# Cutting the weights of the closing products of a triangular inverse to the columns that are used

## Chip, cores and metric

The kernel runs on one core of a Trainium2 chip. The metric is the device time of one execution in microseconds, the median of the runs; the profiled execution is one further run of the same program.

## What is computed

One layer of a hybrid encoder over a prompt of 1024 tokens and a sample of 512. Half of it is a gated delta rule with 8 heads, run once forwards and once backwards over the tokens; the other half is latent attention. The delta rule works in chunks, and within a chunk it solves a unit triangular system:

```python
L = jnp.where(strict, jnp.einsum('bhnid,bhnjd->bhnij', kb, k) * decay, 0.0)
A = L + jnp.eye(CHUNK, dtype=L.dtype)
u = lax.linalg.triangular_solve(A, v * beta[..., None], left_side=True, lower=True, unit_diagonal=True)
w = lax.linalg.triangular_solve(A, kb * jnp.exp(gc)[..., None], left_side=True, lower=True, unit_diagonal=True)
```

After the scan over chunks the two directions are added, normalised and gated; a projection joins both halves, and a norm and the residual close the layer.

## The kernel before

It uses chunks of 128 tokens and forms the inverse of each chunk's triangular matrix explicitly, once per head, chunk and direction. There are 12 jobs: 8 for the prompt (one head, 8 chunks) and 4 for the sample (two heads, 4 chunks each), so 8 slots in each job, times two directions.

A job goes through three generators. `gdn_front` (from line 641) loads keys and queries, forms the decays (`dec`, L673) and the products of keys (`kk`, L681), and writes the strict triangles and the attention weights into the tile `UA` (L686). Its four 32x32 diagonal blocks per slot are inverted by substitution on VectorE, 31 steps of a product and a subtraction (`tm` L737, `XT` L739), and go through DRAM (`dX`) to be spread into block-diagonal matrices.

`gdn_back` (from line 747) reads them back as `dds`, transposes them (`Dp`, L762), so that `Dt` holds the block-diagonal inverse, and multiplies the triangle with it (`Fp`, L773); ScalarE copies the product into the tile `F`. Three rounds follow (lines 780 to 795) which close the inverse from blocks of 32 to 128: `Tt = Dt - F^T Tt`. The first round takes all of the columns; the second takes the 64 columns, and the third the 32 columns, that are not final yet. `cs` are the columns that are computed and `ms` the partitions (rows of the result) that change; which end of the tile they are at depends on the direction. L793 subtracts the partitions `ms` alone. A group is four slots of each direction, so that a round issues eight products, direction 0 first, and a job has two groups. An f32 product appears in the trace as two loads of weights and two matmuls.

`gdn_scan` (from line 799) then carries the state over the chunks: `pk` (L832, L835), `py` (L854), `pu` (L870, L873), with `oacc` (L844, L847, L888) collecting the output.

These generators run as streams beside others: the input projection of the sample (`mm`, L224 to L228), then the preparation of the attention (`pq`), then the attention itself (`s`, `pt`, `po`). `merge` (line 136) interleaves them on TensorE in an order fixed by hand: each stream yields a due time in a clock that `self.cost` (line 116) advances, and the first stream that is due goes next. `cost` is charged with the moving columns of a product, not with its weights. `free` and `hold` keep the PSUM banks of the two directions (`h0`, `h1`) apart in the same clock. The order on the other engines comes from the framework's planner at build time (`schedule_with_timeline_sim`, line 1377), and SyncE issues the DMAs in its own queue.

Of the kernel before, what the change touches and what calls it, by code (L numbers as in the profile page):

```python
# [57 lines left out]
class Kern:  # L58
# [688 lines left out]
    def gdn_back(self, turn, q, T, heads, env, KQ, UA):  # L747

        nc, (gp, cp, psc, dds, dXs) = self.nc, env
        dX = dXs[turn % 2]  # L750
        for items in (((0, 0), (1, 4)), ((0, 4), (1, 0))):
            Ds = {}
            for d, g0 in items:
                src = dX[d].rearrange("(n b) w -> n (b w)", b=4)[g0:g0 + 4, :P * P]
                nc.sync.dma_start(dds[d], src.rearrange("n (r c) -> r n c", c=P))
            yield self.t + 4
            yield from self.free(0, 1)
            for d, g0 in items:
                dd = dds[d]
                ps = psc.tile([P, 4, P], F32, tag=f"h{d}", name="Dp")  # L760
                for i in range(4):
                    nc.tensor.transpose(ps[:, i], dd[:, i], self.ident)  # L762
                    self.cost(P, 2)
                dt2 = cp.tile([P, 4, P], F32, tag="dt2", name="dt2", bufs=2)
                nc.scalar.copy(dt2, ps)
                Ds[d] = (dt2, dd) if d == 0 else (dd, dt2)
            self.hold(HT, 0, 1)
            yield self.t + self.tlat
            yield from self.free(0, 1)
            for d, g0 in items:  # L770
                ps = psc.tile([P, 4, P], F32, tag=f"h{d}", name="Fp")
                for i in range(4):
                    nc.tensor.matmul(ps[:, i], UA[:, d, g0 + i, 0], Ds[d][0][:, i], start=True, stop=True)  # L773
                    self.cost(P, 4)
                F = cp.tile([P, 4, P], F32, tag="F", name="F", bufs=2)
                nc.scalar.copy(F, ps)
                Ds[d] += (F,)
            self.hold(HT, 0, 1)
            yield self.t + self.tlat
            for it, lo in enumerate((0, 64, 96)):  # L780
                yield from self.free(0, 1)
                for d, g0 in items:
                    _, Dt, F = Ds[d]
                    Tt = UA[:, d, g0:g0 + 4, 0]

                    far, near = slice(lo, P), slice(0, P - lo)
                    cs, ms = (far, near) if d == 0 else (near, far)
                    cur = Dt if it == 0 else Tt
                    ps = psc.tile([P, 4, P - lo], F32, tag=f"h{d}", name="Tp")
                    for i in range(4):  # L790
                        nc.tensor.matmul(ps[:, i], F[:, i], cur[:, i, cs], start=True, stop=True)  # L791
                        self.cost(P - lo, 4)
                    nc.vector.tensor_sub(Tt[ms, :, cs], Dt[ms, :, cs], ps[ms])  # L793
                self.hold(HT, 0, 1)
                yield self.t + self.tlat
            if g0 == 4:
                yield
# [595 lines left out]
```

## Time and profile before

| what | value |
|---|---|
| time, median of 3 runs | 3361.96 us |
| lowest and highest run | 3359.56 and 3369.88 us |
| profiled execution: time | 3363.58 us |
| profiled execution: span | 3361.7 us |
| TensorE products, weight loads busy | 3212.2 and 2688.5 us |
| VectorE, ScalarE, GpSimd busy | 1735.1, 1283.6 and 1158.5 us |

The span is the time from the first to the last instruction of the profiled execution. PE stands for TensorE's products, PEld for its loads of weights, which run under the product before; DVE is VectorE, ACT ScalarE, POOL GpSimd, SP SyncE. A product's record is longer than its share of the engine, since products are pipelined: what one costs in a row of many is seen from the distance between starts, or from the chain of work, where each piece ends as the next begins. A form such as 128*32 128x64 gives the rows and columns of weights in use, then the partitions and moving columns.

### The profile page before, as it was taken

Reading aid. Unit: us, or ns where it says so; the run is one execution under the profiler, and the core shown is the slowest. Engines: PE = TensorE matmul, PEld = TensorE weight load, DVE = VectorE, ACT = ScalarE, POOL = GpSimd, SP = SyncE. Lnnn points to the kernel's source line nnn. Section 1 sums busy time; section 2 is a strip of 40 time slices with the busy share of each in tenths; the row PEclk is TensorE's granted clock in tenths of the full one; section 3 lists DMA queues with packets and bytes.
Section 4 is the critical chain, followed back from the end, with each engine's and each line's share of the span. In section 5 each row is a group of like instructions: output and inputs, shape, how many; then the busy total and the mean of one; then the engine's idle time right before and its main releaser. Section 6 shows DMA issues by size and latency. Waiting matters only on the chain.

```text
span 3361.7 us, 46959 instructions
## 1 busy us (share of the span) xinstructions
PE 3212.2 (96%) x16554; PEld 2688.5 (80%) x16554; DVE 1735.1 (52%) x4000; ACT 1283.6 (38%) x2956; POOL 1158.5 (34%) x1026
## 2 busy tenths in 40 slices
PE   8999999999999899999999989899999989999998
PEld 6888888888887688788788777688898878787876
DVE  7234333443412656774775577688787655331212
ACT  4222222222212334444345334365656555432231
POOL 6322222222223532332332334222222444464452
PEclk9999999999999899999999999899999999999999
DMA  4222222222223534334433466522222242564454
GB/s 159 83 73 79 72 78 75 78 72 79 84 75 105 159 100 126 116 107 129 131 111 120 135 211 206 155 82 70 89 76 64 99 135 86 155 186 135 143 168 135
DMA packets 271404, 381.66 MB, mean 114 GB/s; under 512 B 75632, under 2 KB 126824, under 8 KB 269632
## 3 DMA queue, kind: packets, MB, share of 16 engines
q1 hardware_dynamic: 271168, 378.66, 37.0%
q8 instruction: 130, 2.13, 0.3%
q14 instruction: 106, 0.87, 0.1%
HBM read 286.73 MB, written 88.29 MB: 112 GB/s over the span
## 4 chain that ended last, share of the span: by engine, by line
PE 65%; DVE 15%; DMA 10%; issue 3%; ACT 3%; POOL 2%; SPq 1%; POOLq 0%; DVEq 0%; ACTq 0%
PE mm L224 13%; PE mm L228 12%; PE mm L225 12%; DMA wraw<-w_out 3%; PE py L1152 3%; PE py L1151 3%; PE py L1153 3%; DVE tm L737 3%; DVE XT L739 2%; PE Tp L791 2%; POOL wlo L199 2%; PE pt L1074 2%; DMA wraw<-w_in 1%; DVE UA L686 1%; DVE acc L306 1%
## 5 line engine op out<-in xcount | busy, mean ns | idle before, releaser
L199 POOL TENSOR_TENSOR wlo<-wraw,whi 128x512 fp32r<-128x512 f32 x620 | 832.3, 1346 | 1610.4 <-ACT whi L196 1522.3
L224 PE MATMUL mm<-hi,whi 128*128 128x512 f32 x2256 | 910.6, 405 | 16.9 <-ACT whi L196 11.7
L225 PE MATMUL mm<-lo,whi 128*128 128x512 f32 x2256 | 884.7, 393 | 8.1 <-DVE lo L255 8.1
L196 ACT ACTIVATE whi<-wraw 128x512 fp32r<-128x512 f32 x620 | 389.0, 631 | 1181.5 <-PE mm L225 693.4
L228 PE MATMUL mm<-hi,wlo 128*128 128x512 f32 x2256 | 767.5, 394 | 1.6 <-POOL wlo L199 1.5
L224 PEld LDWEIGHTS mm<-hi,whi 128*128 128x128 f32 x2256 | 429.3, 190 | 101.1 <-ACT whi L196 13.7
L228 PEld LDWEIGHTS mm<-hi,wlo 128*128 128x128 f32 x2256 | 427.7, 190 | 97.1 <-POOL wlo L199 5.0
L225 PEld LDWEIGHTS mm<-lo,whi 128*128 128x128 f32 x2256 | 429.4, 190 | 92.7 <-DVE lo L255 10.0
L1151 PE MATMUL py<-whi,mhi 128*128 128x512 f32 x768 | 304.1, 396 | 9.9 <-DVE y L1166 5.6
L1152 PE MATMUL py<-wlo,mhi 128*128 128x512 f32 x768 | 303.8, 396 | 7.5 <-POOL wlo L199 7.4
L1153 PE MATMUL py<-whi,mlo 128*128 128x512 f32 x768 | 302.8, 394 | 0.0
L1035 POOL TENSOR_TENSOR pe<-pe,af 128x512 f32<-128x512 f32 x160 | 166.8, 1060 | 377.8 <-DVE af L1033 203.9
L306 DVE SCALAR_TENSOR_TENSOR acc<-cin,conv_w,acc 128x1024 f32<-128x1024 f32 (+1 forms) x192 | 219.3, 1142 | 40.8 <-ACT acc L304 33.2
L302 DVE TENSOR_TENSOR cin<-mm,rbh 128x512 f32<-128x512 f32 x72 | 47.4, 687 | 311.6 <-PE mm L228 262.6
L1151 PEld LDWEIGHTS py<-whi,mhi 128*128 128x128 f32 x768 | 145.1, 189 | 45.4 <-DVE y L1166 7.5
L1152 PEld LDWEIGHTS py<-wlo,mhi 128*128 128x128 f32 x768 | 145.2, 189 | 44.3 <-POOL wlo L199 12.8
L1153 PEld LDWEIGHTS py<-whi,mlo 128*128 128x128 f32 x768 | 144.8, 189 | 32.3
L310 DVE TENSOR_TENSOR acc<-mm,rbh 128x512 f32<-128x512 f32 x48 | 31.6, 686 | 231.3 <-PE mm L228 231.3
L1166 DVE TENSOR_TENSOR y<-py,g 128x512 f32<-128x512 f32 x36 | 24.7, 690 | 239.1 <-ACT junk L1165 235.7
L1021 ACT ACTIVATE pe<-s,am 128x512 f32<-128x512 f32 x160 | 110.5, 691 | 92.7 <-DVE am L1020 85.6
L737 DVE TENSOR_TENSOR tm<-XT,lam 128x126 f32<-128x126 f32 (+22 forms) x372 | 128.8, 346 | 23.2 <-ACT lam L729 16.1
L199 DVE TENSOR_TENSOR ptl<-pt,pth 128x512 fp32r<-128x512 f32 x160 | 109.9, 687 | 56.9 <-ACT pth L196 55.8
(449 smaller groups left out, 5251.9 us busy)
## 6 DMA issues: line engine op xcount, KB each, us to landing
wraw<-w_in SPq DMA_DIRECT2D x376, 256.0 KB
wraw<-w_out SPq DMA_DIRECT2D x192, 256.0 KB
dd<-dX SPq DMA_DIRECT2D x48, 256.0 KB
wraw<-w_uq SPq DMA_DIRECT2D x36, 256.0 KB
x<-xT_p SPq DMA_DIRECT2D x16, 512.0 KB
xres<-x_p SPq DMA_DIRECT2D x8, 1024.0 KB
y_p<-y SPq DMA_DIRECT2D x32, 256.0 KB
x<-xT_s SPq DMA_DIRECT2D x16, 256.0 KB
```

The lines of the kernel that those rows point to most:

```text
L196: nc.scalar.activation(hi, src, AF.Copy)
L199: (lo_eng or nc.vector).tensor_sub(lo, src, hi.bitcast(F32))
L224: nc.tensor.matmul(ps, whi[:, k], hi[:, s], start=kt == 0, stop=False)
L225: nc.tensor.matmul(ps, whi[:, k], lo[:, s], start=False, stop=False)
L228: nc.tensor.matmul(ps, wlo[:, k], hi[:, s], start=False, stop=kt == KT - 1)
L306: nc.vector.scalar_tensor_tensor(acc, cin[:, j:j + T], w[:, f, j:j + 1], acc, op0=ALU.mult, op1=ALU.add)
L737: nc.vector.tensor_mul(tv, XT[:, :m, j:j + 1].to_broadcast([P, m, n]), lam[j // 16][:, j % 16:j % 16 + 1, j + 1:].to_broadcast([P, m, n]))
L1021: nc.scalar.activation(pe[k], o, AF.Exp, bias=m[:, k:k + 1], scale=-1.0, accum_out=l[:, k:k + 1])
L1035: nc.gpsimd.tensor_mul(pe[k2], pe[k2], f[:, k2:k2 + 1].to_broadcast([P, BLK]))
L1151: nc.tensor.matmul(ps, hi[:, c], w[0], start=kt == kts[0], stop=False)
L1152: nc.tensor.matmul(ps, hi[:, c], w[1], start=False, stop=False)
L1153: nc.tensor.matmul(ps, lo[:, c], w[0], start=False, stop=kt == kts[1] - 1)
```

## The change

The product of the closing rounds takes from `F` only those columns of weights whose results L793 reads, and writes only those partitions of PSUM.

```diff
                     ps = psc.tile([P, 4, P - lo], F32, tag=f"h{d}", name="Tp")
                     for i in range(4):
-                        nc.tensor.matmul(ps[:, i], F[:, i], cur[:, i, cs], start=True, stop=True)
+                        nc.tensor.matmul(ps[ms, i], F[:, i, ms], cur[:, i, cs], start=True, stop=True)
                         self.cost(P - lo, 4)
                     nc.vector.tensor_sub(Tt[ms, :, cs], Dt[ms, :, cs], ps[ms])
```

In the first round `lo` is 0 and `ms` is the whole tile. In the second `ms` has 64 partitions, in the third 32: from partition 0 on for direction 0, and the last ones of the 128 for direction 1.

## Rows read from the trace of the kernel before

**Rows 1.** The page's first part: busy time, share of the span, instructions.
```profile
PE 3212.2 (96%) x16554; PEld 2688.5 (80%) x16554; DVE 1735.1 (52%) x4000; ACT 1283.6 (38%) x2956; POOL 1158.5 (34%) x1026
```

**Rows 2.** Table by stretches: length, busy us and instructions of each engine, clock.
```profile
core 0: us, PE busy (x) PEld busy (x) DVE busy (x) ACT busy (x) POOL busy (x), PEclk, DMA share, GB/s
1200.00:2525.00 1325.00, 1253.91 (x7455) 1076.76 (x7454) 931.45 (x2591) 613.93 (x1676) 409.31 (x395) 0.98 0.41 122
```

**Rows 3.** TensorE's waits from 1200 to 2525 us: total, times, longest.
```profile
PE pk L832 <- DVE oacc L888: 10.5, 9, 3.8
PE py L854 <- DVE oacc L844: 8.8, 12, 2.2
PE py L854 <- ACT oacc L847: 8.1, 9, 2.4
PE pt L1074 <- DVE ptl L199: 5.6, 7, 2.0
PE Fp L773 <- ACT dt L765: 5.1, 2, 3.5
```

**Rows 4.** The chain that ended last, 1200 to 2525 us: shares of the stretch.
```profile
by line: DVE tm L737 6.1%; PE mm L224 5.5%; PE mm L228 5.4%; PE mm L225 5.4%; PE Tp L791 5.3%; DVE XT L739 5.3%; issue 3.8%; DMA wraw<-w_in 2.8%; DVE UA L686 2.5%; DVE acc L306 2.2%; PE Fp L773 1.9%; PE kk L681 1.9%; PE py L854 1.8%; PE pt 
```

**Rows 5.** Groups by line and form, L791: busy us, mean ns | idle before.
```profile
L791 PEld LDWEIGHTS Tp<-UA,F 128*128 128x128 f32 x768 | 91.7, 192 | 4.1 <-DVE z L919 1.1 <-ACT dec L673 0.4 <-DVE UA L793 0.2
L791 PE MATMUL Tp<-UA,F 128*128 128x64 f32 x384 | 45.8, 272 | 0.1
L791 PE MATMUL Tp<-UA,F 128*128 128x32 f32 x384 | 44.9, 271 | 0.7 <-DVE z L919 0.7
```

**Rows 6.** Chain in order of time: start us, us, what; rounds one, two, three.
```profile
1305.09 1.79 PE Tp L791 x16
...
1309.83 1.73 PE Tp L791 x16
...
1314.39 1.71 PE Tp L791 x16
1316.09 0.31 PE mm L224
```

**Rows 7.** Groups by line and form: loads of weights for transposes.
```profile
L762 PEld LDWEIGHTS Dp<-ident,dd 128*128 128x128 f32 x192 | 22.2, 140 | 2.5
...
L491 PEld LDWEIGHTS gtps<-ident,gz 128*32 128x32 f32 x12 | 1.1, 95 | 4.2 <-ACT egls L482 3.0 <-POOL gz L489 0.5
...
L400 PEld LDWEIGHTS crow<-ident,cy 128*8 128x8 f32 x2 | 0.2, 84 | 0.1
```

**Rows 8.** Chain in order of time: products of keys, 256 moving columns.
```profile
1212.71 1.73 PE kk L681 x8
```

**Rows 9.** Timeline of TensorE, four transposes of 64 columns: start us, us, what.
```profile
87.44 0.32 PEld L439 LDWEIGHTS abps<-ident,cacc 64*128 64x128 f32 x4 [0.37 <-issue]
```

**Rows 10.** Timeline of TensorE, and the chain at that time.
```profile
1222.19 1.86 PE L791 MATMUL Tp<-UA,F 128*128 128x32 f32 x16
...
1222.04 1.35 DVE acc L306
```

**Rows 11.** Timeline of TensorE around the transpose into `qcols`.
```profile
889.47 0.61 PE L228 MATMUL mm<-hi,wlo 128*128 128x512 f32 x2
890.02 0.13 PEld L363 LDWEIGHTS qcols<-ident,qrows 64*128 64x128 f32 x1 [0.35 <-issue]
...
890.56 0.40 PE L225 MATMUL mm<-lo,whi 128*128 128x512 f32 x1
```

**Rows 12.** Timeline of TensorE around the transposes into `gtps`.
```profile
117.65 0.39 PE L225 MATMUL mm<-lo,whi 128*128 128x512 f32 x1
117.66 0.32 PEld L491 LDWEIGHTS gtps<-ident,gz 128*32 128x32 f32 x2
117.88 0.38 PE L491 MATMUL gtps<-ident,gz 128*32 128x128 f32 x2
...
118.33 0.40 PE L225 MATMUL mm<-lo,whi 128*128 128x512 f32 x1
```

## What I predict

> **What bounds the kernel now.** I read the shares of the engines first. TensorE's products fill 96% of the span, VectorE 52%, ScalarE 38%, GpSimd 34% [rows 1]. TensorE is the first suspect, but a share averages over stages. So the second view is the table by stretches, cut where the line of the change begins and ends its work: L791 runs from 1201 to 2525 us. In those 1325 us TensorE is busy 1253.9 us, so 71 us are left idle, and VectorE is busy 931.5 us [rows 2]. Two engines are close to full there, so a shorter product need not shorten the stretch. The third view, the list of TensorE's waits in that stretch, says who fills the idle time: the recurrence's products waiting for VectorE (10.5 and 8.8 us) and for ScalarE (8.1 us) lead it [rows 3]. The fourth view, the chain of work that ended last, decides which products count: it passes through VectorE's substitution loop (L737 and L739, 6.1% and 5.3% of the stretch) as much as through TensorE's projections, and through L791 for 5.3% [rows 4], 70 us.
>
> **What the change touches.** L791 is issued by 12 jobs x 2 groups x 3 rounds x 2 directions x 4 slots = 576 products, and the trace has 1152 records, two for each f32 product. The first round (128 columns) is left as it is: `ms` is then the whole of the partitions. Rounds two and three are changed: 384 records with 64 moving columns and 384 with 32 [rows 5]. They stand in bursts of 16 records, 24 bursts of each kind. No operand, wait, DMA or instruction is added, and `self.cost` and so TensorE's own order stays.
>
> **What a burst costs and why.** In the chain, a burst of 16 takes 1.79 us with 128 moving columns, 1.73 with 64 and 1.71 with 32 [rows 6]. Moving a quarter of the columns saves 5%, so the streaming isn't what these records wait for. All have a load of 128 columns of weights of 192 ns [rows 5], the one thing that is equal: a burst goes at the pitch of its loads, about 0.108 us a record (1.73/16).
>
> **What a narrower load costs.** The trace has no load of 64 or 32 columns for a plain f32 product. Its nearest rows are loads for transposes: 140 ns with 128 columns, 95 with 32, 84 with 8 [rows 7]; what doesn't depend on columns is some 82 ns. For the plain load that leaves 192 - 82 = 110 ns in 128 columns, which is the pitch of a burst, and so 0.86 ns a column: 55 ns for 64 columns, 27 for 32 (an estimate by proportion). The next limit is the stream: eight records of 256 columns take 1.73 us [rows 8], 0.216 each, 0.84 ns a column, so 54 ns for 64 columns and 27 for 32. Load and stream then match. The last limit is how fast pairs of load and product follow each other at all. The four transposes into `abps` move 64 columns each; their loads start over 0.32 us, the last one of 0.13 (as a like load in [rows 11]) included, so (0.32 - 0.13)/3 = 0.063 us a pair [rows 9]. That is the closest spacing of a row of such pairs that I found, and whether it is stream or issue that sets it can't be told. So a 64-column record costs 0.055 to 0.063 us; I take 0.060, near the abps row, which has the same stream. A 32-column record costs 0.027 (load and stream) to 0.063 (if the abps spacing is a floor of issue); I take 0.045, the middle, since two mechanisms are equally near.
>
> **The sum.** A burst of 64 falls from 1.73 to 16 x 0.060 = 0.96, by 0.77 us (0.72 to 0.85 by the bounds). A burst of 32 falls from 1.71 to 16 x 0.045 = 0.72, by 0.99 us (0.70 to 1.28). Over all 48 bursts TensorE does 24 x (0.77 + 0.99) = 42 us less.
>
> Not all of it is on the path. In the chain from 1200 to 2525 us there are 15 of the 24 bursts of 1.73 us and 12 of the 24 of 1.70 or 1.71 us (first ones in [rows 6]). The others lie beside VectorE: the 32-column burst at 1222.19 runs while the chain is in `acc` of the convolution, from 1222.04 on for 1.35 us [rows 10]. TensorE would be done earlier there and wait longer for what VectorE hands it. So what counts is 15 x 0.77 + 12 x 0.99 = 11.6 + 11.9 = 23.4 us. With the bounds: 15 x 0.72 + 12 x 0.70 = 19.2 to 15 x 0.85 + 12 x 1.28 = 28.1 us.
>
> The cover of the rest: the 21 bursts off the path cost nothing today because VectorE ends later. If VectorE had less to do there, they would be worth 9 x 0.77 + 12 x 0.99 = 18.8 us more. What is late next on the path is the recurrence behind `oacc` [rows 3], and VectorE's subtraction at L793, which is unchanged. The end of a burst isn't dearer: the projection's full load behind it starts with the last product's stream, as now (the 0.31 us of L224 behind a burst [rows 6] stands). TensorE's order is written out by hand; that of the other engines is made at the build by a planner with a timeline of its own (line 1377). If that timeline sees shorter products, some instructions on VectorE or ScalarE may change places. No row prices that; I leave it at nothing, and the range has room for about 5 us both ways.
>
> The profiled execution took 3363.58 us (span 3361.7), and the median is 3361.96, so the two are 1.6 us apart. 3363.6 - 23.4 = 3340.2 for that execution, 3338.6 against the median; I forecast **3339 us**.
>
> **A product that uses part of the columns may cost a switch.** The trace prices a switch for part of the rows. Between two whole products, the transpose of 64 rows into `qcols` has no load ahead of time (its load starts 0.35 us late, with nothing else waited for), and from the start of the product before it (889.70: the two of L228 end at 889.47 + 0.61, and one lasts 0.38 to 0.39) to that of L225 (890.56) it is 0.86 us [rows 11]. Two whole products at 0.23 and the transpose itself at 0.06 make 0.52; 0.34 us is lost, 0.17 for going in and for coming out. For part of the columns the trace shows nothing of the kind: the two transposes with 32 columns of weights into `gtps` have their load under the product before, and from 117.65 to 118.33 it is 0.68 us, of which two whole products and two transposes of 0.11 (0.38 less the 0.27 of a single one) leave 0 [rows 12]. I go by the latter row, since it is columns that the change cuts, but it is a transpose that writes from the first partition on, while direction 1 writes partitions 64 and 96 onward.
>
> The Trainium skill speaks against the change here (TensorEngine Tiling (Array Packing), Key Properties): "Changing tiling mode (not just tile) drains the TensorE". Of rows the trace agrees, of columns no run here shows it.
>
> **The rivals.** (a) *Each burst pays a switch in and out.* 27 bursts on the path x 0.34 = 9.2 us are given back: 23.4 - 9.2 = 14.2, 3348 us. For it stands qcols, against it gtps. (b) *The whole of TensorE's gain counts*, since VectorE's stretches of the chain begin with something that TensorE hands over earlier: 42 us, 3320 us. For it the 95% busy time in the stretch; against it the 38 us that TensorE already waits for VectorE and ScalarE in the five longest groups of the list [rows 3], which would grow. (c) *Absorbed*: paths almost as long as the chain take over, and under 10 us are left, 3354 us. VectorE and its DMAs hold long pieces of the chain, and nothing on them gets shorter. (d) *Slower*: in a narrow form the load is no longer taken under the product before. Then a record costs its load and its product one behind the other: some 0.055 + 0.27 (a 64-column product's record [rows 5]) = 0.33 us against 0.108, 16 x 0.22 = 3.5 us a burst, 27 on the path 95 us, 3457 us. It turns the sign as soon as the pitch is above 0.108. Against it, gtps again: its second load starts with the first product [rows 12]. That the narrow load takes as long as the full one (the change does nothing) is within (c).
>
> **How the numbers follow.** Chances: forecast 0.44, (a) 0.24, (b) 0.11, (c) 0.15, (d) 0.06. The cases of the forecast, (a) and (c) reach from 3333 to 3356, and (b) pulls the low end down; with 5 us for the planner on the forecast's side I give 3316 to 3358, which leaves out (d), the far half of (b) and a part of (c). About 0.3% (10 us) is what can be told from no change. Faster by more than that, below 3352: nearly all of the forecast and (b), four fifths of (a), a tenth of (c): 0.75. Within it: 0.19. Slower: 0.06.
>
> **What would show it.** Right: weight loads of L791 in two new groups of about 137 and 109 ns, bursts of about 0.96 and 0.72 us between unchanged neighbours, TensorE's busy time down by some 40 us, and its waits for VectorE in the stretch up by 15 to 20. Wrong in the price: bursts that differ from those. A switch shows as a late first load, and 0.15 us or more between the projection's product and the burst's first one. Wrong in the path: bursts as forecast and a span that falls by all of 40 us or by none. The forecast fails altogether if a narrow record's pitch is above 0.108 us.

## The result and the profile after

The changed kernel takes 3328.59 us in the median of its first four runs (3322.42 to 3330.57) against 3360.76 of before, a ratio of 0.9898 with a 95% interval of 0.9873 to 0.9924. A second measurement, below, gave 0.9900 (0.9885 to 0.9916). That is 32 to 34 us, where 23 were forecast: 3339 us was too high by 10, inside the range of 3316 to 3358.

The page's first part of the kernel after (busy us, share of the span, instructions), beside [rows 1]:

```profile
PE 3166.2 (95%) x16554; PEld 2628.6 (79%) x16554; DVE 1739.8 (52%) x4000; ACT 1282.5 (39%) x2956; POOL 1154.3 (35%) x1026
```

TensorE's products have lost 46 us of busy time; VectorE's, ScalarE's and GpSimd's are where they were, to 5 us. The groups by line and form of the kernel after (count, busy us, mean ns) show that the change does what it says; they answer to [rows 5]:

```profile
L791 PE MATMUL Tp<-UA,F 128*64 128x64 f32 x384 | 23.8, 228 | 0.6 <-ACT dec L673 0.4
L791 PE MATMUL Tp<-UA,F 128*32 128x32 f32 x384 | 14.2, 199 | 0.4 <-DVE z L919 0.4
...
L791 PEld LDWEIGHTS Tp<-UA,F 128*64 128x64 f32 x384 | 20.4, 137 | 6.6 <-issue 2.1 <-ACT dec L673 1.0 <-DVE tm L737 0.4
L791 PEld LDWEIGHTS Tp<-UA,F 128*32 128x32 f32 x384 | 11.5, 112 | 7.7 <-issue 1.8 <-DVE XT L739 1.1 <-DVE z L919 0.8
```

The loads fell from 192 ns to 137 and 112, where the working by proportion to the columns gave 137 and 109. What is new stands behind the bar: PEld's idle time before these loads, 4.1 us before the change, is 14.3 us now. The timeline of TensorE of the kernel after (start us, us, what) shows where, first for a burst of 64, then for one of 32:

```profile
1208.71 0.39 PE L228 MATMUL mm<-hi,wlo 128*128 128x512 f32 x1
1209.03 0.97 PE L791 MATMUL Tp<-UA,F 128*64 128x64 f32 x16
1209.93 0.50 PE L224 MATMUL mm<-hi,whi 128*128 128x512 f32 x1
1210.26 0.39 PE L225 MATMUL mm<-lo,whi 128*128 128x512 f32 x1
...
1221.56 0.39 PE L228 MATMUL mm<-hi,wlo 128*128 128x512 f32 x1
1221.88 0.59 PE L791 MATMUL Tp<-UA,F 128*32 128x32 f32 x16
1222.40 0.50 PE L224 MATMUL mm<-hi,whi 128*128 128x512 f32 x1
1222.73 0.39 PE L225 MATMUL mm<-lo,whi 128*128 128x512 f32 x1
...
1209.03 0.83 PEld L791 LDWEIGHTS Tp<-UA,F 128*64 128x64 f32 x16 [0.35 <-ACT whi L196]
```

Take a burst whole, with both of its ends: from the start of the product before it to the start of the second product behind it, less two ordinary products of 0.23. With 64 columns that is 1210.26 - 1208.71 - 0.46 = 1.09 us, with 32 it is 1222.73 - 1221.56 - 0.46 = 0.71. Before, both kinds took 1.79 us, here one with 64 moving columns, 1210.70 - 1208.45 - 0.46:

```profile
1208.45 0.39 PE L228 MATMUL mm<-hi,wlo 128*128 128x512 f32 x1
1208.68 1.89 PE L791 MATMUL Tp<-UA,F 128*128 128x64 f32 x16
1210.38 0.48 PE L224 MATMUL mm<-hi,whi 128*128 128x512 f32 x1
1210.70 0.39 PE L225 MATMUL mm<-lo,whi 128*128 128x512 f32 x1
```

So a burst saves 0.70 and 1.07 us (0.695 and 1.07 without the rounding), and 24 of each 24 x 1.765 = 42.4 us, if the bursts that stand beside other work save as much as those between products of the projection. The first load, which used to go under the product before, comes 0.35 us late. The releaser that the row names, ScalarE's `whi`, is no operand of this load, which reads `F`; the gap is as long as that before `qcols` [rows 11], 0.35.

Where did the 42 us go? The stretch from 1200 us to the last burst holds the same instructions in both kernels, so its length is TensorE's work and its idle time (length, busy us of each engine with instructions; it ends at 2525.1 before, for which [rows 2] has the same row to 0.1 us, and at 2496.6 after):

```profile
1200.00:2496.60 1296.60, 1211.98 (x7456) 1019.47 (x7455) 936.28 (x2591) 612.75 (x1677) 405.11 (x395) 0.98 0.42 125
```

TensorE's busy time went from 1253.9 to 1212.0, 42 us less, as the bursts say (some of it can be the clock: the mean granted clock, of which 1 is the full 2.4 GHz, is 0.983 in the profiled execution before and 0.985 in that after). Its idle time went from 71.1 to 84.6, so 13.5 us were handed back and the stretch is 28.5 us shorter. The other 4.7 of the 33.2 us of span lie behind the last burst, 836.6 us before and 831.9 after, where nothing was changed. A kernel below with all of its weights wide (`swapped`) has 831.5 there too, so these 4.7 us needn't come from the narrow loads. The waits of TensorE in the stretch show who took the 13.5 us (engine, line, whom it waits for: us, times, longest); they answer to [rows 3]:

```profile
PE pk L832 <- DVE oacc L888: 10.2, 14, 2.4
PE py L854 <- DVE oacc L844: 9.7, 12, 2.6
PE py L854 <- ACT oacc L847: 9.2, 7, 3.6
PE pt L1074 <- DVE ptl L199: 7.2, 8, 1.8
PE mm L224 <- ACT whi L196: 5.6, 2, 3.9
```

It is no single wait. The four groups at the head are 33.0 us before and 36.3 after, and the rest comes in pieces of 1 to 4 us, as `mm` behind `whi` here (2.2 us before). Added up over the whole list, TensorE waits for VectorE for 34.2 us before and 38.6 after, for ScalarE for 33.6 and 39.8, and for DMAs and GpSimd for 1.6 and 4.2.

### The profile page after: what moved, and what is told of

Same layout as the page of the kernel before. It is cut to its first block, busy times and chain, and to the rows that moved or that the text cites. A ratio compares the mean times of both kernels' runs of the same rounds, so it can differ in the third digit from the quotient of the medians.

```text
span 3328.5 us, 46972 instructions
## 1 busy us (share of the span) xinstructions
PE 3166.2 (95%) x16554; PEld 2628.6 (79%) x16554; DVE 1739.8 (52%) x4000; ACT 1282.5 (39%) x2956; POOL 1154.3 (35%) x1026
## 4 chain that ended last, share of the span: by engine, by line
PE 28%; DVE 11%; DMA 7%; issue 3%; ACT 2%; POOL 2%; SPq 1%; POOLq 0%; DVEq 0%; ACTq 0%
DMA wraw<-w_out 3%; PE py L1152 3%; PE py L1151 3%; PE py L1153 3%; POOL wlo L199 2%; PE mm L224 2%; PE pt L1074 2%; PE mm L228 2%; PE mm L225 2%; DVE tm L737 2%; DVE XT L739 1%; PE po L1052 1%; PE po L1051 1%; PE po L1053 1%; PE Tp L791 1%
## 5 line engine op out<-in xcount | busy, mean ns | idle before, releaser
L306 DVE SCALAR_TENSOR_TENSOR acc<-cin,conv_w,acc 128x1024 f32<-128x1024 f32 (+1 forms) x192 | 222.3, 1158 | 40.7 <-ACT acc L304 33.6
L1166 DVE TENSOR_TENSOR y<-py,g 128x512 f32<-128x512 f32 x36 | 24.7, 689 | 239.3 <-ACT junk L1165 236.0
```

The lines of the kernel that those rows point to most:

```text
L306: nc.vector.scalar_tensor_tensor(acc, cin[:, j:j + T], w[:, f, j:j + 1], acc, op0=ALU.mult, op1=ALU.add)
```

## Experiments

Three theories of the gain were set against each other. **A**: a fixed set of bursts lies on the path, the 15 and 12 that the chain of before names. **B**: a fixed share, about three quarters, of whatever TensorE saves. **C**: a part of the gain isn't TensorE's but that of the planner, which orders the other engines anew for every program.

**The changed kernel again.** No edit.

> The changed kernel itself, for a narrower interval. In its trace a burst costs, from the start of the projection's product before it to that of the second one behind it and less two ordinary products of 0.23 us, 1.09 us with 64 columns of weights and 0.715 with 32, against 1.786 each before: 24 x (0.695 + 1.07) = 42.4 us of TensorE. Theory A (the bursts that the chain of before names count, 15 and 12 of 24): 15 x 0.695 + 12 x 1.07 = 23.3 us faster than before. Theory B (about three quarters of whatever TensorE saves counts, on or off that chain): 31 to 34 us faster. Theory C (the planner's new order on the other engines gave some 8 us of it): 31 to 34 us too, told from B by the two runs that make half of the change.

Measured: 3330.35 us against 3362.22, a ratio of 0.9900 (0.9885 to 0.9916): 33.6 us faster, 28 to 39 by the interval. The 23.3 us of A are outside it. The gain isn't the clock's: the mean granted clock of these runs is 0.985, that of the kernel before beside them 0.986.

**One round at a time.** Both edits choose, by the round, between the new and the old width (shown against the changed kernel):

```diff
-                        nc.tensor.matmul(ps[ms, i], F[:, i, ms], cur[:, i, cs], start=True, stop=True)
+                        ws = ms if it == 1 else slice(0, P); nc.tensor.matmul(ps[ws, i], F[:, i, ws], cur[:, i, cs], start=True, stop=True)
```

The kernel of round three has `it == 2` there.

> Round two alone is cut to 64 columns of weights; round three stays at 128. TensorE saves 24 x 0.695 = 16.7 us. Theory A: 15 bursts count, 10.4 us faster than before. Theory B: three quarters, 12.5 us. Theory C: the gain isn't tied to what TensorE saves, and this run and the one of round three don't add up to the whole change (off by more than 4 us).

> Round three alone is cut to 32 columns of weights; round two stays at 128. TensorE saves 24 x 1.07 = 25.7 us. Theory A: 12 bursts count, 12.8 us faster than before. Theory B: three quarters, 19 us. Theory C: not tied to it.

Measured: round two alone 3351.06 us, ratio 0.9959 (0.9944 to 0.9973), 13.8 us faster (9 to 19). Round three alone 3341.75 us, 0.9934 (0.9919 to 0.9949), 22.2 us (17 to 27). Burst by burst the saving is as in the whole change (1.09 and 0.715 us). They sum to 36 us against 33.6, so they add up within the noise. They are 83% and 86% of the 16.7 and 25.7 us that TensorE saves, with intervals so wide that all of the saving lies inside both. Round three, with 12 bursts in the chain, speaks against A: 12.8 us are outside its interval. Round two alone doesn't: A's 10.4 us are inside.

**Directions by turns.** In rounds two and three the products of the directions alternate; the subtractions follow as before.

```diff
-                yield from self.free(0, 1)
+                yield from self.free(0, 1); rd = []
...
-                    for i in range(4):
-                        nc.tensor.matmul(ps[ms, i], F[:, i, ms], cur[:, i, cs], start=True, stop=True)
-                        self.cost(P - lo, 4)
-                    nc.vector.tensor_sub(Tt[ms, :, cs], Dt[ms, :, cs], ps[ms])
+                    rd.append((F, Dt, Tt, cur, cs, ms, psc.tile([P, 4, P - lo], F32, tag=f"h{d}", name="Tp")))
+                turns = [(i, r) for i in range(4) for r in rd] if it else [(i, r) for r in rd for i in range(4)]
+                for i, (F, Dt, Tt, cur, cs, ms, ps) in turns:
+                    nc.tensor.matmul(ps[ms, i], F[:, i, ms], cur[:, i, cs], start=True, stop=True)
+                    self.cost(P - lo, 4)
+                    if i == 3: nc.vector.tensor_sub(Tt[ms, :, cs], Dt[ms, :, cs], ps[ms])
```

> The changed kernel, with the eight products of rounds two and three issued by turns, direction 0 and direction 1, instead of four and four. Theory: products of the two directions, which use different columns of the array, run side by side, as three of each already do where the directions meet in the changed kernel. Then a burst of 16 records takes the time of 8 pitches and a switch in and out: 8 x 0.0585 + 0.345 = 0.81 us (1.09 before this) with 64 columns, 8 x 0.0315 + 0.345 = 0.60 us (0.715) with 32; TensorE saves another 24 x (0.28 + 0.115) = 9.5 us, and the time falls by 5 to 8 us below the changed kernel. Rival: what meets at the border is an effect of two queues and not of the array, or one load at a time is all that the engine takes; then bursts stay at 1.09 and 0.715 and the time at that of the changed kernel, within 3 us.

Timeline of TensorE in this kernel, a burst of 64 and one of 32:

```profile
1207.30 0.39 PE L228 MATMUL mm<-hi,wlo 128*128 128x512 f32 x1
1207.62 0.69 PE L791 MATMUL Tp<-UA,F 128*64 128x64 f32 x16
1208.23 0.50 PE L224 MATMUL mm<-hi,whi 128*128 128x512 f32 x1
1208.57 0.39 PE L225 MATMUL mm<-lo,whi 128*128 128x512 f32 x1
...
1219.86 0.39 PE L228 MATMUL mm<-hi,wlo 128*128 128x512 f32 x1
1220.18 0.45 PE L791 MATMUL Tp<-UA,F 128*32 128x32 f32 x16
1220.56 0.50 PE L224 MATMUL mm<-hi,whi 128*128 128x512 f32 x1
1220.89 0.39 PE L225 MATMUL mm<-lo,whi 128*128 128x512 f32 x1
```

The mechanism is right. A burst is 1208.57 - 1207.30 - 0.46 = 0.81 us, as expected, and 1220.89 - 1219.86 - 0.46 = 0.57, below the 0.60 expected; TensorE saves another 24 x (0.28 + 0.15) = 10.3 us. The time doesn't follow: 3332.82 us, 0.9906 (0.9890 to 0.9921) of before, where the changed kernel has 0.9900; by the intervals, a gain of more than 5 us is unlikely.

Two things that may have taken up a part of it can be read from the runs. The first is waiting. In the stretch TensorE is idle for 90.0 us, 5 us more than the changed kernel, and its waits for VectorE add up to 44.8 us, 6 more. The second is the granted clock: its mean over the five runs by turns is 0.9834, over the four runs of the changed kernel beside them 0.9852. At the lower level, 1.2 GHz, ordinary products start 0.43 us apart, not 0.23. The table of the stretch, one of a piece at the lower level, and two products from that piece, all of the kernel by turns:

```profile
1200.00:2494.90 1294.90, 1204.92 (x7450) 1010.78 (x7449) 933.89 (x2590) 611.90 (x1674) 407.47 (x394) 0.98 0.42 125
2135.00:2152.10 17.10, 13.09 (x47) 8.88 (x48) 8.63 (x18) 5.19 (x15) 2.55 (x2) 0.50 0.49 150
...
2138.35 0.63 PE L965 MATMUL kp<-cl,whi 128*128 128x512 f32 x1
2138.78 0.63 PE L966 MATMUL kp<-ch,wlo 128*128 128x512 f32 x1
```

A mean that is 0.0018 lower means 0.0036 of 3330 us, or 12 us, more at the lower level. If TensorE always had work then, that costs 12 x (1 - 0.23/0.43) = 5.6 us (an estimate from these rows, at the most). No run holds the clock, so its share of the missing 10 us isn't shown.

**The other order of directions, wide weights.** The kernel before, with direction 1 ahead in rounds two and three.

```diff
-                for d, g0 in items:
+                for d, g0 in items[::-1] if it else items:
...
-            if g0 == 4:
+            if items[-1][1] == 4:
```

> The kernel before, wide weights, with direction 1 issued ahead of direction 0 in rounds two and three. TensorE's work, burst by burst, is the same to 0.01 us, but the planner sees another input and orders VectorE, ScalarE and SyncE differently in places. Theory B (the gain is TensorE's saving): the time of before within 2 us. Theory C (the planner's order moves the time by as much as the surplus of the gain): 4 to 10 us from before, to either side.

Measured: 3369.61 us, 1.0019 (1.0008 to 1.0030): 6.4 us *slower* (3 to 10), with TensorE's work unchanged. Its stretch, to the last burst at 2538:

```profile
1200.00:2538.00 1338.00, 1252.89 (x7455) 1076.18 (x7454) 932.27 (x2591) 612.98 (x1676) 407.35 (x395) 0.98 0.41 121
```

TensorE is busy for 1252.9 us, as in [rows 2], and idle for 85.1: 14 us more, as much as the whole change handed back. Its order on TensorE differs only within the bursts, while the line numbers of VectorE's sequence, position by position, differ from those of before at 158 of 4000 places and ScalarE's at 12 of 2956. (The change itself moves far more: 1004 and 91.) So a build with the same work on TensorE can differ by 6 us in time, as C says and B doesn't. What moves it isn't separated: the planner's order, the direction whose result is ready first, and the granted clock all differ. The mean clock is 0.9836 over these 11 runs and 0.9849 over the 15 of before beside them, which by the working above is worth up to some 4 of the 6.4 us.

**With less on VectorE.** Before, after and by turns, each without steps 16 to 30 of the substitution (left out of the computation in all three):

```diff
-        for j in range(31):
+        for j in range(16):
```

> The kernel before without steps 16 to 30 of the substitution on VectorE (left out of the computation), some 372 - 180 = 192 fewer pairs of L737 and L739, 192 x 0.67 = about 129 us of VectorE's 1735. It is the base of the next two. If VectorE bounds parts of the stretch, it is itself faster than before, by 20 us or more; if TensorE alone does, by under 10 us.

> The changed kernel without steps 16 to 30 of the substitution (left out of the computation). Theory B with VectorE as what absorbs the rest: with VectorE out of the way all of TensorE's 42 us count, 38 to 43 us below the base without these steps. Theory A (a fixed set of bursts lies on the path): near 23 us. If what absorbs the rest isn't VectorE (transfers, GpSimd, or the recurrence itself), the difference stays at the 32 us of the whole kernels.

> The kernel with the directions by turns, without steps 16 to 30 of the substitution (left out of the computation). With the whole substitution the turns saved 24 x (0.283 + 0.147) = 10.3 us of TensorE and nothing of the time. If VectorE took that up, 8 to 10 us below the changed kernel without these steps; if it is something else, again within 3 us of it.

Measured: 3332.04 us (3330.09 to 3335.36), 3296.17 (3291.39 to 3300.64) and 3295.77 (3293.45 to 3299.53). The base is 31 us faster than the whole kernel before (ratio 0.9910, 0.9895 to 0.9926), so VectorE does set a part of the time. On this base the change brings 35.9 us, with some 8 us of uncertainty either way by the two intervals: it can be told neither from the 32 to 34 on the whole one nor from the 42 of TensorE. The turns bring nothing that can be told from zero again, where 8 to 10 were expected if VectorE's substitution took them up. The stretch of the base:

```profile
1200.00:2495.10 1295.10, 1237.56 (x7442) 1068.03 (x7441) 838.55 (x2262) 609.98 (x1672) 408.04 (x394) 0.99 0.41 125
```

And of the changed kernel without these steps:

```profile
1200.00:2463.30 1263.30, 1199.74 (x7457) 1017.48 (x7456) 845.67 (x2261) 610.92 (x1677) 406.32 (x395) 0.98 0.43 128
```

TensorE's idle time goes from 57.5 to 63.6 us, 6 us handed back where it was 13.5. That suggests that the substitution is a part of what absorbs TensorE's gain; since the time doesn't show it beyond the noise, and only half of the steps were left out, how large a part isn't shown.

**Time given back.** The changed kernel with each narrow product issued twice:

```diff
-                        nc.tensor.matmul(ps[ms, i], F[:, i, ms], cur[:, i, cs], start=True, stop=True)
+                        [nc.tensor.matmul(ps[ms, i], F[:, i, ms], cur[:, i, cs], start=True, stop=True) for _ in range(2 if it else 1)]
```

> The changed kernel with each product of rounds two and three issued twice, the second over the first. A burst grows by 16 records of 0.0585 or 0.0315 us: from 1.09 to 2.03 us and from 0.715 to 1.22; TensorE gets back 24 x (0.936 + 0.504) = 34.6 of the 42.4 us. Theory B (about three quarters of TensorE's work in these bursts counts): 24 to 28 us above the changed kernel, 4 to 9 below before. Theory A (15 and 12 bursts on the path): 15 x 0.936 + 12 x 0.504 = 20 us above. Theory C (a good part of the gain is the planner's order and isn't tied to TensorE): 10 to 16 us above, or nothing that fits.

Timeline of TensorE, the ends of a burst of 64:

```profile
1207.16 0.39 PE L228 MATMUL mm<-hi,wlo 128*128 128x512 f32 x1
1207.48 1.90 PE L791 MATMUL Tp<-UA,F 128*64 128x64 f32 x32
...
1209.64 0.39 PE L225 MATMUL mm<-lo,whi 128*128 128x512 f32 x1
```

A burst is 1209.64 - 1207.16 - 0.46 = 2.02 us, so 16 more records cost 0.93, 0.058 each; for round three it is 1.22, and 16 more cost 0.51, 0.032 each. Time: 3345.61 us, 0.9950 (0.9936 to 0.9964). TensorE does 24 x (1.79 + 1.79 - 2.02 - 1.22) = 8 us less than before, and the kernel is 16.8 us faster (12 to 22), where B said 4 to 9. Against the changed kernel, 34.6 us more work cost 15 us by the medians and 17 by the ratios: C's 10 to 16 or just above. By the two intervals it can be 10 to 24, so A's 20 isn't excluded, and B's 24 to 28 hardly.

**The planner's other mode.** Before and after with

```diff
-    with tile.TileContext(nc, schedule_with_timeline_sim=True) as tc:
+    with tile.TileContext(nc, schedule_with_timeline_sim=False) as tc:
```

> The kernel before with the planner's other mode at line 1377, which orders VectorE, ScalarE, GpSimd and SyncE by another timeline. It is the base of the next one; slower than before by 0 to 100 us, nothing hangs on how much.

> The changed kernel with that other mode of the planner. Theory B: 28 to 36 us below the base with the same mode, as with the first mode. Theory C: the gain depends on which order the planner makes, and comes out 8 us or more from 32. Theory A, with a chain of its own: 20 to 26.

Measured: 3428.18 us (3419.78 to 3431.60) and 3403.53 (3391.86 to 3405.64), so 24.7 us between them, with the same bursts (1.786 to 1.09 and 0.715). That is 58% of TensorE's saving, with some 8 us of uncertainty either way by the two intervals, so none of the three theories is excluded by it.

**65 columns.** Direction 0 takes 65 columns in rounds two and three, direction 1 all 128:

```diff
-                        nc.tensor.matmul(ps[ms, i], F[:, i, ms], cur[:, i, cs], start=True, stop=True)
+                        ws = slice(0, 65) if d == 0 and it else slice(0, P); nc.tensor.matmul(ps[ws, i], F[:, i, ws], cur[:, i, cs], start=True, stop=True)
```

> Direction 0 of rounds two and three takes 65 columns of weights from partition 0 on (one more than half of the array, and for round three 33 more than are read); direction 1 stays at 128. If the late first load of a burst comes with a product that uses 64 or 32 columns of the array, it is absent here: the loads of direction 0 go at 0.0585 us as with 64 columns, a burst is 8 x 0.112 + 8 x 0.0585 = 1.36 us with its ends as before, in both rounds. If any load of fewer than 128 columns makes it, a burst is about 1.66 us. In time 20 or 6 us of TensorE, some 15 or 5 us.

Timeline of TensorE in this kernel:

```profile
1209.30 0.40 PE L228 MATMUL mm<-hi,wlo 128*128 128x512 f32 x1
1209.54 1.53 PE L791 MATMUL Tp<-UA,F 128*65 128x64 f32 x16
1210.87 0.48 PE L224 MATMUL mm<-hi,whi 128*128 128x512 f32 x1
1211.19 0.39 PE L225 MATMUL mm<-lo,whi 128*128 128x512 f32 x1
...
1209.30 1.62 PEld L791 LDWEIGHTS Tp<-UA,F 128*65 128x65 f32 x16
```

The first load starts at 1209.30, together with the product before it, and nothing is late. A burst is 1211.19 - 1209.30 - 0.46 = 1.43 us, nearer to the 1.36 of no switch than to the 1.66 of one. So a narrow load by itself has no switch; it comes with products confined to 64 or 32 columns. In round three, which moves 32 columns here, a burst is just as long, 1224.33 - 1222.45 - 0.46 = 1.42:

```profile
1222.45 0.40 PE L228 MATMUL mm<-hi,wlo 128*128 128x512 f32 x1
1222.68 1.50 PE L791 MATMUL Tp<-UA,F 128*65 128x32 f32 x16
...
1224.33 0.39 PE L225 MATMUL mm<-lo,whi 128*128 128x512 f32 x1
```

So with 65 columns loaded it is the load that sets the pitch, not the columns that are moved. Its time, 3344.11 us, is of a single run and isn't used.

## Why the prediction was right, and where it was off

**What bounds a burst: right.** The pitch of the loads set it; the kernel with 65 columns, whose burst is as long with 32 moving columns as with 64, leaves out the stream. With the narrow loads a record costs 0.058 us with 64 columns, in the range of 0.055 to 0.063 and next to the 0.060 taken. With 32 it costs 0.032, near the low end of 0.027 to 0.063 and not the 0.045 in the middle: the spacing of the `abps` transposes [rows 9], 0.063, is no floor of issue for these products.

**The switch: wrong step, right bound.** I went by `gtps` [rows 12], which shows none. By the turns, where nothing else is left, a burst is 0.81 - 8 x 0.058 = 0.34 us more than its pitches with 64 columns and 0.57 - 8 x 0.032 = 0.31 with 32. That is close to the 0.34 us of `qcols` [rows 11]. Not all of it need be the switch: the burst with 65 columns, where no load is late, is 0.07 us more than its pitches too (1.43 against 8 x 0.112 + 8 x 0.058 = 1.36), which leaves 0.27 and 0.24. So rival (a) is there in each of the 48 bursts, 24 x 0.51 to 24 x 0.65 = 12 to 16 us of TensorE in all. The rule of the Trainium skill (TensorEngine Tiling (Array Packing), Key Properties), that a change of tiling mode drains TensorE, agrees with the 0.35 us late loads of the bursts. `gtps`, which is a transpose, isn't a witness for plain products; why it shows no switch stays open.

**What made up for it.** I had the two directions one behind the other. In the changed kernel 16 records take 0.97 - 0.23 = 0.74 us from first to last start, less than 15 x 0.058 = 0.87, and by turns 0.69 - 0.22 = 0.47, eight pitches: products in different columns of the array run side by side, a few where the directions meet, all of them by turns. Nor was the burst before 1.73 or 1.71 us long: with both of its ends it is 1.79. The length before, the pitch of round three, switch and overlap together left 0.70 + 1.07 for the 0.77 + 0.99 us forecast, 42.4 us for 42. The sum over TensorE was right because these errors cancel, and that is luck.

**The path: off.** 23.4 of 42 us were to count, since the chain holds 27 of 48 bursts [rows 4, 6, 10]. In the stretch 28 counted, and its idle time rose by 13.5 us. The forecast had 15 to 20 us more of waits for VectorE alone; these rose by 4.4 us, and those for ScalarE by 6.2, so it isn't VectorE alone that hands things over late. 5 us more came from behind the stretch. Rival (c) held for the turns, whose 10 us didn't show in the time; (d) didn't come. The 32 to 34 us measured lie midway between the 23.4 of the forecast and the 42 of (b), inside the range because its low end had been drawn towards (b). That the change pays and that a good part stays in waits was right, but the 55% isn't a property of the bursts that the chain names: the change as a whole gives 76% to 79%, the one-round kernels 83% and 86%, the planner's other mode 58%, each of the last three with an uncertainty of about a fifth of the saving or more, either way.

**What stays open.** The forecast left the planner's order at nothing, "about 5 us both ways". The swapped directions show 6.4 us between two builds with the same work on TensorE, up to some 4 of them by the clock, and the doubled products 9 us more gain than work. The surplus of 9 to 10 us over the forecast is about as large. How much of it is order, how much the clock and how much the chain's undercount isn't settled: no run holds the order of all engines, or the clock, while the products change. Nor was it shown what takes up the time that the turns save: waits for VectorE and the clock can each hold a part, but with less work on VectorE the turns gained nothing either.

## What to carry to other kernels

In this kernel a row of small f32 products costs the load of its weights when no more columns are moved than loaded (0.112 us a record with 128 loaded, 0.058 with 64, 0.032 with 32); so cut the columns of weights to those whose results are read, and look in the trace whether the pitch is the load's. Count the switch in and out of a narrow form for each burst, and let products in different columns alternate. On an engine that is 95% busy, expect a part of its saving in the time (here between a half and four fifths), and don't read a difference of 6 us between two builds as the effect of an edit when a planner orders the other engines anew; compare the granted clock of the two first.

## What was not expected of the hardware

A burst confined to 64 or 32 columns of the array pays about a quarter to a third of a us for the switch in and out (0.24 to 0.34), while with 65 columns no load is late, and two transposes with 32 columns [rows 12] lose nothing. Products that use different columns start side by side: 16 records of 64 columns in 0.47 us by turns, where one direction alone needs 0.058 for each. And in the changed kernel this begins by itself where the directions meet, although eight records of direction 0 are issued ahead of the first of direction 1: 0.74 us from first to last start instead of 0.87.
